# One step of a linked chain to a block of products, and its small products queued behind that block

## The chip, the core and the metric

The kernel runs on one core of a Trainium2 chip. The metric is the device time of one execution in microseconds (us), from runs of the whole program; a separate execution is recorded by the hardware profiler. A core has five engines with instruction queues of their own: TensorE (PE: matrix products and transposes; its weight loads are listed apart as PEld), VectorE (DVE), ScalarE (ACT), GpSimd (POOL) and SyncE (SP), which issues most of the transfers here. Products land in PSUM, from where VectorE and ScalarE read them. The profile also shows the clock that TensorE was granted, as a share of full speed.

## What is computed

One layer of a hybrid sequence model on a float32 input of 2048 positions by 1024 channels, with 16 learned positions put in front (T = 2064). Three groups of heads read one common projection; a gated feed-forward part follows. Cut to what matters:

```python
p = rms_norm(h, norm_mix_pre) @ w_in                  # (T, 1024) @ (1024, 3080)
oa = rg_lru_group(...)                                # linear recurrence, 256 channels
ob = forgetting_attention_group(...)                  # 8 heads of 64, causal softmax with decay
oc = rwkv7_group(...)                                 # 4 heads of 64, matrix-valued state
h = h + rms_norm(concat([oa, ob, oc]) @ w_out, norm_mix_post)
f = causal_dwconv(rms_norm(h, norm_ffn_pre) @ ffn_up, ffn_conv)
gate, val = split(f, 2)
h = h + rms_norm((gelu(gate) * val) @ ffn_down, norm_ffn_post)

# rwkv7_group, at each position, for each head:
s_kk = S @ kk_t
S = S * w_t - outer(s_kk, kk_t * a_t) + outer(v_t, k_t)
o_t = S @ r_t
```

The last three lines are the recurrence that the change is about. The kernel computes it in chunks of 64 positions: within a chunk the dependence of the positions on each other is a triangular 64 x 64 system, whose inverse is built up from 16 x 16 blocks to 32 x 32 and to 64 x 64 by small products; only one 64 x 64 state a head passes from chunk to chunk.

## The kernel before

**Stages.** The first stage makes the input projection (L226 w_in_step): each operand is split into a high and a low part, and `mm3` (L172) adds three products for each of 8 slices of the 1024 channels, so that one *block of products* is 24 products, of 128 output columns by 256 to 400 positions. The positions are taken in three parts of two blocks each; in every part 24 groups of 128 columns are gone through, thus 48 blocks of products a part and 144 in all, after a small product for the attention gates at the head of each part. Attention, the output projection, the feed-forward up projection and the down projection follow.

**Work beside the blocks.** The LRU group and the RWKV recurrence are written as Python generators, and the main loop calls `beside.advance()` (L2171) after each block of products, which traces some of their steps there. `Beside` (L2040) adds PACE = 1.25 to what is due at each call, and takes steps until less than one is due: one step a block, two after every fourth. The generators begin after the 26th block of the first part, and a third of their work is added in each part at the same place. What is left when the first stage ends is traced without any blocks (`finish`), while attention follows.

**Steps of the recurrence.** `recurrences` (L2070) goes through 9 blocks of 256 positions (the last has 64), three in each part. For each: four steps of preparation, in `block` and the head of `chunks` (L1112) (decays, keys, scores, transposes); then the triangular solve of the 16 x 16 blocks, 15 alternations of GpSimd and VectorE; then the *ending* of the block before it; then four steps of `lru_block` (L1412). An ending has ten steps:

1. load the solved 16 x 16 blocks (`xt`) and transpose them (`xr`);
2. u1: products of the scores with `xr`, masked by VectorE (L1212);
3. x1: products of `xt` with u1, added up by VectorE (L1219), and further products for the diagonal 32 x 32 blocks (L1226);
4. u2: products of the scores with x1, copied by VectorE (L1233);
5. `xf`: products with u2, copied by ScalarE (L1238);
6. to 10. products for the 64 x 64 systems (L1244, L1254), the state from chunk to chunk (L1269 to L1293), the outputs (L1320, L1325) and their norm, and the output (L1345), which is stored for the next stage.

Steps 2 to 5 are linked: each product needs what VectorE made of the product before. All of the four use the helper `small` (L1201), whose name stands in the trace as L1202: 32 x 32 products. A float32 product of this kind shows as two instructions in the trace. For a block of four chunks u1 has 64 of them, x1 32 (and 64 for the diagonal blocks), u2 32 and `xf` 32. The products of the recurrence take turns in two PSUM buffers (`rps`), those of the preparation and of the LRU group share one more (`eps`), and the blocks of products have five (`psp`).

**What sets the order.** Every engine works through its own queue in order. The order in these queues is fixed when the program is built: a scheduler goes through the traced instructions with a simulated clock, and an instruction that was traced earlier goes first among those that it holds to be ready. `tc.issue_after(i)` puts the instructions traced under it behind instruction `i` in the queue of its engine; it makes no wait of its own.

Of the kernel before, what the change touches and what calls it, by code (L numbers as in the profile page):

```python
# [20 lines left out]
KD = D // P  # L21
# [150 lines left out]
def mm3(nc, out, ah, al, bh, bl, first, last, more=False):  # L172

    nc.tensor.matmul(out, ah, bh, start=first, stop=False, skip_group_check=more)  # L174
    nc.tensor.matmul(out, ah, bl, start=False, stop=False, skip_group_check=more)  # L175
    nc.tensor.matmul(out, al, bh, start=False, stop=last, skip_group_check=more)  # L176

# [48 lines left out]
def w_in_step(core, pools, psum, weights, block, kind, c0, scr):  # L226

    nc = core.nc
    wh, wl = weights
    st = pools["st"]  # L230
    t0, n, tl, hi, lo = block
    ps = psum.tile([P, 512], F32, tag="mm", name=core.n("psp"))
    for k in range(KD):
        mm3(nc, ps[:, :n], wh[:, k], wl[:, k], hi[:, k], lo[:, k], k == 0, k == KD - 1)
    if kind in ("q", "k"):
        sc = 0.125 if kind == "q" else 1.0
# [209 lines left out]
class Attn:  # L446
# [537 lines left out]
class Rwkv:  # L984
# [3 lines left out]
    BLOCKS = 9  # L988
    SOLVED = "solved"

    @staticmethod
# [120 lines left out]
    def chunks(self, b, nch, sg, rav, bk, wc, bon):  # L1112
# [3 lines left out]
        nc, k, core = self.nc, self.k, self.core  # L1116
# [4 lines left out]
        sc = self.t([P, ni, 192], "sc", bufs=2)  # L1121
# [71 lines left out]
        nc.vector.transpose(xr.rearrange("p i s -> p (i s)"), xt.rearrange("p i s -> p (i s)"))  # L1193
        yield

        xf = self.t([64, ni, 64], "xf")
        nc.gpsimd.memset(xf[32:64, :, 0:32], 0.0)
        groups = [(i0, min(16, ni - i0)) for i0 in range(0, ni, 16)]
        m1 = k["mask1"][:].rearrange("p (o t) -> p o t", o=1)

        def small(o, lhsT, rhs, lo_out, lo_in):  # L1201
            nc.tensor.matmul(  # L1202
                o[lo_out : lo_out + 32], lhsT[lo_in : lo_in + 32], rhs[lo_in : lo_in + 32], start=True, stop=True,
                tile_position=(lo_in, lo_out),
            )

        for i0, m in groups:
            ps = self.ps().rearrange("p (i t) -> p i t", t=32)
            for i in range(m):
                for q in (0, 32):  # L1210
                    small(ps[:, i], sc[:, i0 + i, 128 + q : 160 + q], xr[:, i0 + i], q, q)
            tt(u1[:, i0 : i0 + m], ps[0:64, :m], m1.to_broadcast([64, m, 32]), op=ALU.mult)  # L1212
        yield
        for i0, m in groups:
            g = slice(i0, i0 + m)
            ps = self.ps().rearrange("p (i t) -> p i t", t=32)
            for i in range(m):
                small(ps[:, i], xt[:, i0 + i], u1[:, i0 + i], 0, 0)
            tt(x1[0:32, g], ps[0:32, :m], xr[0:32, g], op=ALU.add)  # L1219
            ps = self.ps().rearrange("p (i t) -> p i t", t=32)  # L1220
            for i in range(m):
                for q in (0, 32):
                    small(ps[:, i], u1[:, i0 + i], xt[:, i0 + i], q, q)
            for q in (0, 32):
                qs = slice(q, q + 32)
                tt(xf[qs, g, q : q + 32], ps[qs, :m], xt[qs, g], op=ALU.add)  # L1226
        yield
        for i0, m in groups:
            g = slice(i0, i0 + m)
            ps = self.ps().rearrange("p (i t) -> p i t", t=32)  # L1230
            for i in range(m):
                small(ps[:, i], sc[:, i0 + i, 160:192], x1[:, i0 + i], 32, 0)
            nc.vector.tensor_copy(u2[32:64, g], ps[32:64, :m])  # L1233
            yield
# [4 lines left out]
        yield  # L1239
        for i0 in range(0, ni, 8):  # L1240
# [6 lines left out]
            nc.scalar.activation(w3[0:64, i0 : i0 + m, 64:128], ps[0:64, :m], AF.Copy)  # L1247
        yield
        ap = self.t([P, 2, ni, 64], "xu")[0:64, 0]
        for i0 in range(0, ni, 4):  # L1250
# [5 lines left out]
            nc.scalar.activation(w3[0:64, i0 : i0 + m, 0:64], ps[0:64, :m, 64:128], AF.Copy)  # L1256
        yield
        gt, rp = self.t([P, m2, CH], "gt"), rav[:, :, 0]
# [26 lines left out]
        for c in range(nch):  # L1285
# [7 lines left out]
            nc.vector.tensor_copy(st[:, c + 1], gain[:, c])  # L1293
        yield

# [42 lines left out]
        tt(on.rearrange("p q a (h t) -> p (q a) h t", h=2), v4(od), r14, op=ALU.mult)  # L1338
        yield
        n = CH * nch  # L1340
# [20 lines left out]
        )  # L1361
        yield

# [675 lines left out]

class Beside:  # L2040


# [6 lines left out]
    def step(self):  # L2049
        while self.gens:  # L2050
            try:
                next(self.gens[0])
                return True
            except StopIteration:
                self.gens.pop(0)
        return False

    def advance(self):
        self.due += self.pace if self.gens else 0.0
        while self.due >= 1.0:  # L2060
            self.due -= 1.0
            if not self.step():
                break
# [316 lines left out]
```

## Time and profile before

| | |
|---|---|
| median of three runs | 2995.25 us (2985.94 to 2998.46) |
| profiled execution | 2996.0 us, its recorded span 2994.3 us |
| granted TensorE clock, mean | 0.976 |
| block products (L174 to L176 on psp) | 3 x 1152, 1136.6 us busy |
| TensorE's work on the recurrence's buffers (rps), 42 to 878.5 us | 161.1 us (2897 instructions) |
| the same, 878.5 to 1125 us | 82.1 us (1266 instructions) |
| waits of GpSimd for VectorE in the solve (L1178) | 67.5 us, 99 times |

Busy time of TensorE is the time in which at least one product runs; products overlap, so the sum over groups can be above it. A line such as `L1202 ... rps<-rwxu,rwsc 32*32 32x32 f32 x32 [1.46 <-DVE rwxu L1219]` gives start, duration, engine, source line, what is written from which tiles, the shape of the stationary and of the moving operand, a count of merged instructions, and in brackets the idle time of the engine before it and whose result ended it. In a list of waits the numbers are the total, how often, and the longest. The stretches that a table of windows shows are cut from the start of the span.

### The profile page before, as it was taken

What the parts mean: (1) busy time and instruction counts of PE and PEld (TensorE: products, weight loads), DVE (VectorE), ACT (ScalarE), POOL (GpSimd) and SP (SyncE); (2) the same over time, 40 slices, a digit from 0 to 9 for tenths busy, and PEclk for the clock granted to TensorE, in tenths of its full rate; (3) what the DMA queues carried; (4) which work ended last, traced back from release to release, by engine and by line L of the source; (5) the groups of instructions that cost most, each with busy time, mean ns of one, the idle gap of its engine ahead of it and who ended that gap; (6) DMA issues with size and microseconds to landing.
All of it is one profiled execution on the core that took longest, in us unless ns stands there. A gap on an engine that the chain in (4) does not pass through costs nothing.

```text
span 2994.3 us, 52802 instructions
## 1 busy us (share of the span) xinstructions
PE 2898.0 (97%) x18694; PEld 2486.3 (83%) x18694; DVE 2037.0 (68%) x3937; ACT 1480.8 (49%) x2858; POOL 1319.7 (44%) x1567
## 2 busy tenths in 40 slices
PE   6999999999999999999999999999999999999998
PEld 6998899888886655665568999999999999787887
DVE  5258644765677776565636998898778787656766
ACT  4246332443346554455634656666565665424333
POOL 1002122121223665666843667446655544656443
PEclk9999899999988999999999999999999999999999
DMA  6777469676644347544336565577777764436453
GB/s 210 239 235 226 135 230 310 203 242 194 199 129 101 95 109 208 134 113 109 77 96 212 183 198 179 173 220 211 208 208 218 222 198 128 158 116 220 145 174 120
DMA packets 469190, 530.49 MB, mean 177 GB/s; under 512 B 85710, under 2 KB 355736, under 8 KB 467372
## 3 DMA queue, kind: packets, MB, share of 16 engines
q1 hardware_dynamic: 468156, 526.17, 58.2%
q8 instruction: 147, 2.41, 0.3%
q0 software_dynamic: 768, 0.93, 0.1%
q14 instruction: 119, 0.97, 0.1%
HBM read 368.07 MB, written 158.90 MB: 176 GB/s over the span
## 4 chain that ended last, share of the span: by engine, by line
PE 59%; DVE 4%; POOL 2%; DMA 2%; ACT 2%; issue 2%; SPq 0%; DVEq 0%; POOLq 0%; ACTq 0%
PE psu L174 9%; PE psu L175 9%; PE psu L176 9%; PE po L716 4%; PE psd L174 4%; PE psd L175 4%; PE psd L176 4%; PE mx L566 2%; PE pswo L174 2%; PE pswo L176 2%; PE pswo L175 2%; PE sc L693 2%; PE sc L694 2%; POOL acc L737 1%; DVE mc L571 1%
## 5 line engine op out<-in xcount | busy, mean ns | idle before, releaser
L175 PE MATMUL psu<-xo,uw 128*128 128x344 f32 x1848 | 591.4, 320 | 0.0
L174 PE MATMUL psu<-xo,uw 128*128 128x344 f32 x1848 | 586.0, 322 | 2.7 <-ACT u L1828 1.2
L176 PE MATMUL psu<-xo,uw 128*128 128x344 f32 x1848 | 581.9, 320 | 1.3 <-POOL uw L1657 1.0
L174 PE MATMUL psp<-xh,wh 128*128 128x384 f32 (+2 forms) x1152 | 380.8, 331 | 0.0
L176 PE MATMUL psp<-xh,wl 128*128 128x384 f32 (+2 forms) x1152 | 378.0, 328 | 0.0
L175 PE MATMUL psp<-xl,wh 128*128 128x384 f32 (+2 forms) x1152 | 377.8, 328 | 0.0
L1657 DVE TENSOR_TENSOR uw<-uq,uw 128x512 fp32r<-128x512 f32 x341 | 320.3, 944 | 59.2 <-ACT uw L1656 56.7
L174 PEld LDWEIGHTS psu<-xo,uw 128*128 128x128 f32 x1848 | 345.8, 188 | 4.3 <-DVE vb L1848 1.8
L176 PEld LDWEIGHTS psu<-xo,uw 128*128 128x128 f32 x1848 | 345.7, 188 | 2.1 <-POOL uw L1657 1.3
L175 PEld LDWEIGHTS psu<-xo,uw 128*128 128x128 f32 x1848 | 347.1, 188 | 0.0
L1656 ACT ACTIVATE uw<-uq 128x512 fp32r<-128x512 f32 x462 | 287.9, 627 | 95.7 <-PE psu L176 44.4
L698 ACT ACTIVATE p<-sc,bias 128x512 f32<-128x512 f32 (+4 forms) x352 | 197.9, 590 | 142.3 <-PE sc L694 119.2
L571 DVE TENSOR_REDUCE mc<-mx 128x1 f32<-128x512 f32 (+6 forms) x352 | 190.0, 565 | 113.6 <-PE mx L566 80.1
L1796 DVE SCALAR_TENSOR_TENSOR uy<-psu,ffn_cols,uy 128x342 f32<-128x342 f32 (+1 forms) x390 | 220.4, 567 | 61.4 <-ACT uy L1794 59.7
L1804 POOL TENSOR_TENSOR uy<-uy,uy 128x342 f32<-128x342 f32 (+1 forms) x132 | 146.5, 1110 | 229.2 <-DVE uy L1796 55.9
L737 POOL TENSOR_TENSOR acc<-acc,p 128x512 f32<-128x512 f32 (+3 forms) x208 | 222.7, 1073 | 48.4 <-DVE acc L737 23.4
L1657 POOL TENSOR_TENSOR uw<-uq,uw 128x512 fp32r<-128x512 f32 x121 | 184.4, 1524 | 133.8 <-ACT uw L1656 116.0
L174 PEld LDWEIGHTS psp<-xh,wh 128*128 128x128 f32 x1152 | 220.1, 191 | 8.7 <-issue 7.3
L176 PEld LDWEIGHTS psp<-xh,wl 128*128 128x128 f32 x1152 | 220.1, 191 | 7.0 <-issue 5.1
L175 PEld LDWEIGHTS psp<-xl,wh 128*128 128x128 f32 x1152 | 220.1, 191 | 5.0 <-issue 3.2
L1657 DVE TENSOR_TENSOR fo<-u,fo 128x896 fp32r<-128x896 f32 x88 | 101.6, 1155 | 133.7 <-ACT fo L1656 133.2
L1656 ACT ACTIVATE fo<-u 128x896 fp32r<-128x896 f32 x88 | 81.2, 923 | 206.6 <-PE psd L176 118.1
(488 smaller groups left out, 6409.4 us busy)
## 6 DMA issues: line engine op xcount, KB each, us to landing
uq<-scr_us SPq DMA_DIRECT2D x220, 256.0 KB
uq<-in_ffn_up_dram SPq DMA_DIRECT2D x209, 256.0 KB
wl<-scr_wk SPq DMA_DIRECT2D x48, 512.0 KB
wh<-scr_wk SPq DMA_DIRECT2D x48, 512.0 KB
u<-scr_ff SPq DMA_DIRECT2D x88, 256.0 KB
scr_ff<-uy SPq DMA_DIRECT2D x110, 171.0 KB
raw<-in_w_in_dram SPq DMA_DIRECT2D x24, 512.0 KB
scr_wk<-wh SPq DMA_DIRECT2D x24, 512.0 KB
```

The lines of the kernel that those rows point to most:

```text
L174: nc.tensor.matmul(out, ah, bh, start=first, stop=False, skip_group_check=more)
L175: nc.tensor.matmul(out, ah, bl, start=False, stop=False, skip_group_check=more)
L176: nc.tensor.matmul(out, al, bh, start=False, stop=last, skip_group_check=more)
L566: nc.tensor.matmul(ps[:rows, : e - a], q3[:, qo : qo + rows], k2[:, a:e], start=True, stop=not last)
L571: self.reduced = nc.vector.tensor_reduce(mc[:rows, i, ci : ci + 1], ps[:rows, : e - a], axis=AX.X, op=ALU.max)
L698: last = nc.scalar.activation(p[:rows, :w], ps[:rows, :w], AF.Exp, bias=bias[:rows, j : j + 1])
L716: mm = nc.tensor.matmul(po[at : at + 64, c0:n], v1[:rows, j], p[:rows, : n - c0], start=start and i < 2, stop=end and i + 2 >= len(group), ...
L737: eng.tensor_tensor(a, ps_[0][0][:rows, c0:n] if start and i == 1 else a, p[:rows, : n - c0], op=ALU.add)
L1656: core.nc.scalar.activation(hi, src, AF.Copy)
L1657: (eng or core.nc.vector).tensor_tensor(lo, src, hi, op=ALU.subtract)
L1796: core.conved = stt(y[:, :n], src[:, i : n + i], cw[:, 44 * i + cc : 44 * i + cc + 1], y[:, :n], op0=ALU.mult, op1=ALU.add)
L1804: core.pooled = nc.gpsimd.tensor_tensor(v[:, :n], g[:, :n], v[:, :n], op=ALU.mult)
```

## The change

The generators' ending returns a mark, FAR, at each of its yields. `advance` takes at most two steps at a call, and stops after a step that returned the mark. The three linked products u1, x1 and u2 are put behind the last product of the block of products that was traced before them; for that, `mm3` returns its last instruction and `w_in_step` keeps it. No instruction is added or removed on any engine. The other nine places where a plain `yield` becomes `yield self.FAR` are left out.

```diff
@@ mm3
-    nc.tensor.matmul(out, al, bh, start=False, stop=last, skip_group_check=more)
+    return nc.tensor.matmul(out, al, bh, start=False, stop=last, skip_group_check=more)
@@ w_in_step
-        mm3(nc, ps[:, :n], wh[:, k], wl[:, k], hi[:, k], lo[:, k], k == 0, k == KD - 1)
+        core.produced = mm3(nc, ps[:, :n], wh[:, k], wl[:, k], hi[:, k], lo[:, k], k == 0, k == KD - 1)
@@ class Rwkv
     SOLVED = "solved"
+    FAR = "far"
@@ chunks
         nc.vector.transpose(xr.rearrange("p i s -> p (i s)"), xt.rearrange("p i s -> p (i s)"))
-        yield
+        yield self.FAR
...
+        behind = lambda: core.tc.issue_after(core.produced.ins)
...
                 for q in (0, 32):
-                    small(ps[:, i], sc[:, i0 + i, 128 + q : 160 + q], xr[:, i0 + i], q, q)
+                    with behind():
+                        small(ps[:, i], sc[:, i0 + i, 128 + q : 160 + q], xr[:, i0 + i], q, q)
...
             for i in range(m):
-                small(ps[:, i], xt[:, i0 + i], u1[:, i0 + i], 0, 0)
+                with behind():
+                    small(ps[:, i], xt[:, i0 + i], u1[:, i0 + i], 0, 0)
...
             for i in range(m):
-                small(ps[:, i], sc[:, i0 + i, 160:192], x1[:, i0 + i], 32, 0)
+                with behind():
+                    small(ps[:, i], sc[:, i0 + i, 160:192], x1[:, i0 + i], 32, 0)
...
@@ class Beside
+    MOST = 2
...
     def step(self):
         while self.gens:
             try:
-                next(self.gens[0])
-                return True
+                return next(self.gens[0]) or True
             except StopIteration:
                 self.gens.pop(0)
         return False

     def advance(self):
         self.due += self.pace if self.gens else 0.0
-        while self.due >= 1.0:
+        for _ in range(self.MOST):
+            if self.due < 1.0:
+                break
             self.due -= 1.0
-            if not self.step():
+            if self.step() in (False, Rwkv.FAR):
                 break
```

More of the change, by code (lines that the diff above doesn't have):

```diff
@@ L1210, in chunks @@
                 for q in (0, 32):
-                    small(ps[:, i], sc[:, i0 + i, 128 + q : 160 + q], xr[:, i0 + i], q, q)
+                    with behind():
+                        small(ps[:, i], sc[:, i0 + i, 128 + q : 160 + q], xr[:, i0 + i], q, q)
             tt(u1[:, i0 : i0 + m], ps[0:64, :m], m1.to_broadcast([64, m, 32]), op=ALU.mult)
-        yield
+        yield self.FAR
         for i0, m in groups:
@@ L1226, in chunks @@
                 tt(xf[qs, g, q : q + 32], ps[qs, :m], xt[qs, g], op=ALU.add)
-        yield
+        yield self.FAR
         for i0, m in groups:
@@ L1231, in chunks @@
             for i in range(m):
-                small(ps[:, i], sc[:, i0 + i, 160:192], x1[:, i0 + i], 32, 0)
+                with behind():
+                    small(ps[:, i], sc[:, i0 + i, 160:192], x1[:, i0 + i], 32, 0)
             nc.vector.tensor_copy(u2[32:64, g], ps[32:64, :m])
-            yield
+            yield self.FAR
             ps = self.ps().rearrange("p (i t) -> p i t", t=32)
@@ L1238, in chunks @@
             nc.scalar.activation(xf[0:32, g, 32:64], ps[0:32, :m], AF.Copy)
-        yield
+        yield self.FAR
         for i0 in range(0, ni, 8):
@@ L1247, in chunks @@
             nc.scalar.activation(w3[0:64, i0 : i0 + m, 64:128], ps[0:64, :m], AF.Copy)
-        yield
+        yield self.FAR
         ap = self.t([P, 2, ni, 64], "xu")[0:64, 0]
@@ L1256, in chunks @@
             nc.scalar.activation(w3[0:64, i0 : i0 + m, 0:64], ps[0:64, :m, 64:128], AF.Copy)
-        yield
+        yield self.FAR
         gt, rp = self.t([P, m2, CH], "gt"), rav[:, :, 0]
@@ L1293, in chunks @@
             nc.vector.tensor_copy(st[:, c + 1], gain[:, c])
-        yield
+        yield self.FAR
         ntl = -(-nch // 2)
@@ L1338, in chunks @@
         tt(on.rearrange("p q a (h t) -> p (q a) h t", h=2), v4(od), r14, op=ALU.mult)
-        yield
+        yield self.FAR
         n = CH * nch
@@ L1361, in chunks @@
         )
-        yield
+        yield self.FAR
 def lru_consts(core, pool, psum, w):
```

## The prediction

> **What bounds the kernel now.** I read the page first (engines, clock row), then the stretches of the first stage, then TensorE's waits there, then the instructions around the longest of them. Columns of the stretches: bounds and length, then busy us (count) of TensorE, its weight loads, VectorE, ScalarE and GpSimd, the granted clock, DMA share, GB/s.
>
> ```profile
> span 2994.3 us, 52802 instructions
> PE 2898.0 (97%) x18694; PEld 2486.3 (83%) x18694; DVE 2037.0 (68%) x3937; ACT 1480.8 (49%) x2858; POOL 1319.7 (44%) x1567
> PEclk9999899999988999999999999999999999999999
> ```
>
> TensorE is the bound, over the whole span. What the change can win is TensorE's idle time and the time at a lowered clock; it removes no product.
>
> ```profile
> 42.00:878.50 836.50, 820.16 (x6809) 755.60 (x6808) 488.42 (x1181) 338.58 (x647) 140.53 (x218) 0.97 0.67 214
> 878.50:1125.00 246.50, 227.67 (x1982) 154.37 (x1983) 185.44 (x514) 137.78 (x297) 131.87 (x206) 0.86 0.45 106
> 289.60:317.00 27.40, 25.70 (x253) 20.88 (x246) 24.18 (x70) 17.28 (x33) 9.69 (x14) 0.50 0.25 83
> 405.70:412.60 6.90, 6.54 (x47) 6.47 (x48) 3.51 (x8) 0.00 (x0) 0.32 (x1) 0.51 0.10 30
> 671.90:678.80 6.90, 6.49 (x49) 4.97 (x50) 6.53 (x15) 3.62 (x8) 2.36 (x5) 0.51 0.42 133
> 767.50:771.00 3.50, 3.50 (x20) 3.47 (x17) 2.94 (x8) 1.00 (x4) 0.50 (x1) 0.51 0.65 186
> 317.00:878.50 561.50, 551.02 (x5121) 502.71 (x5120) 333.93 (x831) 215.16 (x425) 116.91 (x179) 0.98 0.66 213
> ```
>
> Blocks of products run from 42 to 878.5 us. There TensorE idles 836.5 - 820.2 = 16.3 us, and the clock is 0.97. From 878.5 to 1125 the recurrence's rest runs beside attention: 18.8 us idle, clock 0.86. The half-speed stretches inside the first stage are the four small ones above (among others): one where the first third of the stage meets the second (289.6 to 317), and three of 6.9, 6.9 and 3.5 us.
>
> ```profile
> PE rps L1202 <- DVE rwxu L1219: 6.1, 4, 2.5
> PE pst L145 <- DVE xl L152: 2.0, 1, 2.0
> 401.49 2.21 PE L1202 MATMUL rps<-rwxu 32*32 32x32 f32 x96
> 406.06 1.91 PE L1202 MATMUL rps<-rwxu,rwsc 32*32 32x32 f32 x32 [1.46 <-DVE rwxu L1219]
> 407.90 0.69 PE L174 MATMUL psp<-xh,wh 128*128 128x384 f32 x1
> 408.39 0.52 PE L175 MATMUL psp<-xl,wh 128*128 128x384 f32 x1
> ...
> 412.73 0.34 PE L174 MATMUL psp<-xh,wh 128*128 128x384 f32 x1
> 412.91 0.33 PE L175 MATMUL psp<-xl,wh 128*128 128x384 f32 x1
> ...
> 563.88 1.19 PE L1202 MATMUL rps<-rwxu,rwsc 32*32 32x32 f32 x32 [0.38 <-DVE rwxu L1219]
> 672.31 1.91 PE L1202 MATMUL rps<-rwxu,rwsc 32*32 32x32 f32 x32 [2.47 <-DVE rwxu L1219]
> 766.41 1.19 PE L1202 MATMUL rps<-rwxu,rwsc 32*32 32x32 f32 x32 [1.80 <-DVE rwxu L1219]
> 859.14 1.19 PE L1202 MATMUL rps<-rwxu,rwsc 32*32 32x32 f32 x32
> ```
>
> The largest wait of the stage after 302 us is the linked chain: the product u2 (the 32 recorded instructions with rwsc) needs the sum x1 that VectorE makes (L1219) from the product ahead of it. It waits four times, in blocks 1 to 4 of the recurrence, 1.46, 0.38, 2.47 and 1.80 us; in block 5 (859.14) it doesn't. Each of the three long ones opens one of the half-speed stretches: the block products behind it take 0.52 us (start to start 0.32) against 0.34 (0.175) further on.
>
> ```profile
> 403.45 0.75 DVE L1458 TENSOR_TENSOR_SCAN rwlu<-rwla,lru_h,rwlg 128x256 f32<-128x256 f32 x1
> 405.34 0.67 DVE L1219 TENSOR_TENSOR rwxu<-rps,rwxu 32x512 f32<-32x512 f32 x1
> 408.10 0.67 DVE L1233 COPY rwxu<-rps 32x512 f32<-32x512 f32 x1
> ```
>
> Why is x1 late? Its product starts at 401.49, its sum only at 405.34: VectorE works through the LRU group's steps (L1458 and its neighbours) first.
>
> **The change part by part.** mm3 now returns its last product, and w_in_step keeps it as core.produced: no instruction, 0 us. Beside.step hands on the value FAR, advance takes at most MOST = 2 steps, and none after one that returned FAR. With 1.25 steps due at each block of products, before, each fourth block took two; I counted both orders through by hand, from block of products 26, where the recurrence begins, to 144, the last. After a FAR step the debt is carried (up to 3.0 steps) and paid back in the LRU and the next block's front, two steps at a time. Both orders leave the same 28 steps over at the end of the stage, so the work behind 878.5 us is the same. Of the three linked products u1, x1, u2 of a block of the recurrence, only these stood two to a block of products: u1 and x1 of block 1, x1 and u2 of blocks 3 and 5. The LRU steps move one or two blocks of products later (block 2's from 58-60 to 60-61, block 4's from 99-101 to 101-102). No DMA is added; the transfers in the steps (xt's loads, the store of mix) move with them by at most three blocks of products on SP's queue.
>
> The second part queues u1 (64 recorded instructions), x1 (32) and u2 (32) behind the last product traced before them. What does that hold back? I compare where each stood when it was traced with where it ran, by the block products that had started by then (24 to a block).
>
> ```profile
> 42.00:395.90 353.90, 272.74 (x1448) 258.18 (x1448) 20.02 (x36) 18.98 (x39) 0.96 0.66 213
> 42.00:552.60 510.60, 399.31 (x2101) 373.58 (x2101) 31.59 (x57) 26.31 (x54) 0.96 0.71 230
> 42.00:659.70 617.70, 464.70 (x2478) 430.65 (x2478) 37.80 (x69) 31.27 (x65) 0.97 0.70 227
> 42.00:756.40 714.40, 525.01 (x2920) 486.20 (x2920) 41.57 (x78) 34.65 (x74) 0.97 0.69 222
> 42.00:848.50 806.50, 585.85 (x3348) 540.88 (x3348) 48.67 (x95) 38.83 (x85) 0.97 0.68 219
> ```
>
> These stretches count block products alone, up to the start of u1 of blocks 1 to 5: 1448/24 = 60.3, 87.5, 103.3, 121.7 and 139.5 blocks. Traced they are after 51, 79, 94, 106 and 128. So u1 runs 8 to 16 blocks of products later than its place in the program, because the chain of the recurrence (each step waits for a PSUM buffer and for VectorE) is slower than the pace. A rule that holds it behind block 51 (or x1 behind 52 instead of 51) binds nothing at block 60. I cost the queueing at 0; the cover that hides it is this lag, and without it a linked product would be at most one block later: 24 products at the 0.175 us start to start seen above, 4.2 us.
>
> Does splitting the pairs shorten the waits? The trace holds the answer in part: block 4's three products are already traced one to a block (106, 107, 108), as the change wants, and its u2 still waits 1.80 us and is followed by 3.5 us at half clock; block 5's x1 and u2 are a pair and u2 doesn't wait at all. What is late next after x1 is VectorE's queue, not the order of TensorE's. Bounds: at most all of it goes, 6.1 us of waits and half of the stretches of 6.9 + 6.9 + 3.5 us, 8.6: 14.7 us won. On the other side, each of some 15 linked products before 878.5 us (three in each of five blocks) comes 4.2 us later, 63 us of chain that run behind 878.5 instead. What does a us of chain cost there? The tail loses 18.8/246.5 = 0.08 to idling and 0.14 to the clock, the stage from 317 on 0.02 and 0.02: 0.18 more. 63 x 0.18 = 11 us lost. Between these I take the row nearest to a split trio, block 4: a wait of 1.8 and half of 3.5, 3.5 us. Block 1 (1.46 + 3.45 = 4.9) and block 3 (2.47 + 3.45 = 5.9) come down to that: 1.4 + 2.4, about 4 us won.
>
> The stretch from 289.6 to 317 I leave as it is. The blocks of the first third are done by then and the norms of the second third feed no products yet, so there is no block for the recurrence's products to stand behind. The LRU steps moved by a block or two run beside blocks that keep TensorE busy; were they to meet the next linked sum on VectorE, they cost one more wait like the four, 0.4 to 2.5 us.
>
> The Trainium skill, "TensorE: Matmul & The Clock Gate", section "Why this matters for your kernels", puts the loss of the clock at idle gaps beyond some 3 us between bursts. Here the clock halves after gaps of 1.46, 2.47 and 1.80 us with sparse 32x32 products around them, so the trace is stricter than the rule. By the rule the change could win only the 6.1 us of waits, by the rows up to 14.7.
>
> The sum: the profiled execution took 2996.0 us, 1.7 beyond its span of 2994.3; 2996.0 - 4 = 2992. It lies 0.7 us above the median of the three times shown (2995.25), so against that I forecast **2991**.
>
> **The rivals.** *It works as it says* (2978): a whole block then stands between two linked products wherever the stage has blocks, the four waits and their half-speed stretches go (14.7), and the small products beyond 302 us at the first seam, spread likewise, give back half of what the half clock costs between 302 and 317, a quarter of 15 us (about 3.5). 18 us in all, from 2996.0. For it: each long wait opens a half-speed stretch, so one cause takes both. Against it: the lag of 8 to 16 blocks, and block 4.
>
> *The chain falls back* (3013): u1, x1 and u2 are held until a block has been issued, VectorE's LRU work meets them there, and a whole period of the recurrence (u1 of block 4 to u1 of block 5 is 848.5 - 756.4 = 92 us) slides behind 878.5. At 0.18 us each us that is 17 us, 2996.0 + 17. It decides from 15/0.18 = 83 us of added chain, some 14 us or three and a half blocks in each of six periods. For it: the tail is the worst place for this chain, clock 0.86. Against it: the same 28 steps are left over, and the queueing is slack.
>
> *It doesn't do what it says*: the order on TensorE comes out the same and the time stays at 2995; this lies inside my own case.
>
> **How the numbers follow.** My forecast with the unchanged order 0.44, 2991, own range 2984 to 2999. It works: 0.36. The chain falls back: 0.20. What a measurement here can tell from no change is about 0.5%, 15 us: faster means below 2980, slower above 3010. Nearly all of the second case lies below (0.34 with what strays), the third above but for a little, together with mishaps of the first 0.21; within 0.45. The range reaches to the middle of both rivals and leaves out 0.1 on each side: 2974 to 3012.
>
> **What would show it.** The recurrence's last transposes stand so far in this row (their first and last start):
>
> ```profile
> L1345 PE MATMUL rps<-ident,rwxu x2: 364/365/366, 1119.5 to 1121.4; 64*128 64x64 f32 x2
> ```
>
> Right: u1 of block 1 still near 60 blocks of products, waits of L1202 for L1219 of 4 to 6 us in the stage, clock 0.97 there, those transposes still near 1121 us. Wrong on the fast side: those waits below 1 us and a clock of 0.99 beyond 317 us. Wrong on the slow side: more than 83 us of the recurrence's chain moved past the last block, or a stage that ends later than 878.5. The forecast rests on the lag; if a changed place in the program changes the order of the engines' queues more widely, it fails there.

## The result, and the profile after

The changed kernel takes 3005.37 us (median of nine runs, 2999.9 to 3012.64). The kernel before, run beside it, takes 2994.27 us (nine runs, 2985.94 to 3000.02). The ratio is 1.0041 with a 95% interval of 1.0029 to 1.0053: 0.41% slower. The forecast, 2991 us, lay on the other side; the range, 2974 to 3012, holds the time.

The page of the changed kernel, in the first two rows that were shown of before:

```profile
span 3010.9 us, 52805 instructions
PE 2902.7 (96%) x18694; PEld 2489.5 (83%) x18694; DVE 2029.8 (67%) x3937; ACT 1484.6 (49%) x2858; POOL 1320.1 (44%) x1567
```

TensorE is busy for 4.7 us more with the same 18,694 instructions. The profiled execution took 3012.64 us, the longest of the nine runs; that of before took 2995.96, near its median. So 16.7 us are to be found between the two, of which some 11 are typical.

Stretches of the changed kernel (columns as in the prediction). The first has the bounds that were used for before. The others are cut at its own marks: from the first block product to the start of the 55th block of products, from there to the last block product, from there to the recurrence's last product, and from there to attention's last product (`po`).

```profile
42.00:878.50 836.50, 819.33 (x6797) 755.87 (x6796) 482.56 (x1177) 340.19 (x646) 142.37 (x220) 0.97 0.66 214
...
41.77:354.77 313.00, 307.62 (x2045) 287.95 (x2045) 175.79 (x405) 132.00 (x237) 26.00 (x45) 0.97 0.66 211
354.77:876.62 521.85, 510.06 (x4744) 466.63 (x4743) 305.66 (x770) 207.56 (x408) 114.82 (x174) 0.97 0.67 217
...
876.60:1134.30 257.70, 229.59 (x1998) 155.79 (x1997) 187.25 (x514) 137.84 (x297) 128.62 (x204) 0.86 0.42 100
1134.30:1554.10 419.80, 405.88 (x1833) 238.75 (x1832) 245.07 (x489) 212.99 (x386) 287.39 (x374) 0.98 0.46 117
```

The same marks in the kernel before:

```profile
42.15:361.46 319.31, 313.45 (x2045) 292.88 (x2045) 175.93 (x406) 130.33 (x236) 27.95 (x45) 0.95 0.65 208
361.46:877.96 516.50, 506.02 (x4763) 462.26 (x4763) 312.23 (x776) 208.21 (x411) 112.58 (x173) 0.98 0.68 219
...
878.00:1121.90 243.90, 225.52 (x1977) 153.27 (x1977) 184.43 (x507) 135.18 (x293) 130.80 (x205) 0.86 0.45 106
1121.90:1538.40 416.50, 404.24 (x1833) 237.86 (x1833) 245.29 (x490) 213.97 (x388) 287.04 (x375) 0.98 0.47 118
```

The reader is to see that the first stage did not get longer in these two executions (its last block product starts at 876.6 instead of 878.0 us), but that two changes of opposite sign hide in this: the changed kernel gains 6.3 us up to the 55th block of products, at the seam of the first two thirds, and loses 5.4 from there to the last. The stretch in which the rest of the recurrence runs beside attention got longer: 257.7 - 243.9 = 13.8 us, of which TensorE idles 28.1 - 18.4 = 9.7 more. Attention behind it took 3.3 us more, and what follows attention is equal within 1 us. The work left behind the stage is the same: TensorE is busy on the recurrence's buffers for 82.25 us after the last block product, before 82.26.

Inside the stage, the longest of TensorE's waits, the products u2 of blocks 1 to 5, four of which wait for x1 (now L1205 and L1224; the lines of the ending stand 3 to 6 lower than before), and the recurrence's last transposes:

```profile
PE rps L1205 <- DVE rwxu L1224: 8.8, 4, 3.5
```

```profile
403.94 1.35 PE L1205 MATMUL rps<-rwxu,rwsc 32*32 32x32 f32 x32 [2.75 <-DVE rwxu L1224]
558.00 1.66 PE L1205 MATMUL rps<-rwxu,rwsc 32*32 32x32 f32 x32 [1.19 <-DVE rwxu L1224]
669.82 1.91 PE L1205 MATMUL rps<-rwxu,rwsc 32*32 32x32 f32 x32 [3.49 <-DVE rwxu L1224]
766.13 1.61 PE L1205 MATMUL rps<-rwxu,rwsc 32*32 32x32 f32 x32 [1.36 <-DVE rwxu L1224]
...
865.17 1.35 PE L1205 MATMUL rps<-rwxu,rwsc 32*32 32x32 f32 x32
```

```profile
L1351 PE MATMUL rps<-ident,rwxu x2: 364/365/366, 1130.2 to 1132.9; 64*128 64x64 f32 x2
```

The waits that a split was to shorten grew: 1.46, 0.38, 2.47 and 1.80 us became 2.75, 1.19, 3.49 and 1.36, in sum 8.8 for 6.1. Two more executions with the order of before have 6.7 (e1) and 7.8 us (e5), one more with the order of the change 11.1 (e6); up to the end of the stage the queues of these are the same as in the pair.

For blocks 2 and 3 the reason stands in TensorE's order. So many block products are queued between the start of x1 and the start of u2:

| block of the recurrence | 1 | 2 | 3 | 4 | 5 |
|---|---|---|---|---|---|
| before | 4 | 16 | 18 | 2 | 16 |
| with the change | 4 | 4 | 6 | 3 | 16 |

The rule traces x1 and u2 one block of products (24) apart in all five, but the queue has 3 to 6 between them in the first four, fewer than before. One block apart in the program is not one block apart in the queue: the scheduler places these products 8 to 16 blocks of products later than they were traced, by its own clock. So TensorE has less to do while VectorE makes the sum. At block 1 the count is the same; there the sum itself starts 5.1 us after x1 (398.08 us) instead of 3.9, with VectorE at LRU steps until then. Executions spread here too: with the order of before, e1 and e5 wait 2.21 and 2.10 us at block 1, not 1.46.

What VectorE does in that time also changed at the longest wait, block 3. Here are the four engines around it in the changed kernel: SyncE's issue of an LRU load, ScalarE, VectorE, TensorE.

```profile
662.96 0.47 SPq L1432 DMA_DIRECT2D rwlraw<-scr_p  x1
...
667.27 0.60 ACT L1439 ACTIVATE rwlu<-rwlraw,lru_cols 128x256 f32<-128x256 f32 x1 [4.52 <-DMA rwlraw<-scr_p]
...
669.18 0.42 ACT L1462 ACTIVATE rwlr<-rwlr 128x256 f32<-128x256 f32 x1
...
667.91 0.51 DVE L1441 SCALAR_TENSOR_TENSOR rwlu<-rwlraw,lru_cols,rwlu 128x256 f32<-128x256 f32 x1 [4.40 <-ACT rwlu L1439]
669.09 0.67 DVE L1224 TENSOR_TENSOR rwxu<-rps,rwxu 32x512 f32<-32x512 f32 x1
...
661.71 2.21 PE L1205 MATMUL rps<-rwxu 32*32 32x32 f32 x96
```

The product x1 starts at 661.71 and takes 2.21 us, but its sum L1224 runs only at 669.09. VectorE isn't busy for most of it: it stands still for 4.40 us at the head of its queue, at an LRU instruction that needs ScalarE, and ScalarE stands still for 4.52 us at an LRU load that was issued at 662.96. The linked sum is queued behind both. ScalarE in the kernel before, at the same two instructions:

```profile
663.46 0.42 ACT L1456 ACTIVATE rwlr<-rwlr 128x256 f32<-128x256 f32 x1
...
665.92 0.60 ACT L1433 ACTIVATE rwlu<-rwlraw,lru_cols 128x256 f32<-128x256 f32 x1
```

The instruction that waits (L1433, now L1439) is the first of the LRU group's block 5. It is traced only after some 115 blocks of products, but the scheduler holds it ready and puts it here, near block 104. Before, it stood behind the square root that ends block 4's gates (L1456, now L1462), and its load, issued at 661.29, had landed when it was due. The rule traces block 4's LRU steps two blocks of products later (their first gate products run at 646.34 instead of 640.54 us); so block 5's first instruction now stands ahead of block 4's square root, and the 4.3 us from its load's issue to its start lie open.

That this order made the wait longer is not shown here. The product x1 of the kernel before, and u2 of the same block in e5, which has the order of before:

```profile
664.25 2.21 PE L1202 MATMUL rps<-rwxu 32*32 32x32 f32 x96
...
670.04 1.19 PE L1202 MATMUL rps<-rwxu,rwsc 32*32 32x32 f32 x32 [3.49 <-DVE rwxu L1219]
```

Before, u2 started 672.31 - 664.25 = 8.06 us after x1, with the change 669.82 - 661.71 = 8.11: the sum was as late, behind other work of VectorE, and only TensorE had more to do (18 block products instead of 6). In e5 the wait is 3.49 us as well, without the rule. And over the whole kernel the first instructions of the LRU blocks (L1433, now L1439) wait for transfers 35.7 us in 15 cases, before 33.0 in 12.

A wait of the same kind stands behind the stage. TensorE, then ScalarE in the changed kernel:

```profile
909.17 0.79 PE L693 MATMUL sc<-q,k 128*128 128x512 f32 x1 [5.56 <-ACT p L698]
...
908.62 0.35 ACT L1026 ACTIVATE rwwa<-rwraw,rwkv_om 128x64 f32<-128x64 f32 x1 [5.78 <-DMA rwraw<-scr_p]
908.87 0.25 ACT L698 ACTIVATE p<-sc,bias 16x16 f32<-16x16 f32 x1
```

and ScalarE at that instruction in the kernel before:

```profile
905.45 0.35 ACT L1025 ACTIVATE rwwa<-rwraw,rwkv_om 128x64 f32<-128x64 f32 x1 [1.58 <-DMA rwraw<-scr_p]
```

An exponential of attention (L698) stands behind a preparation step of the recurrence's last block, whose operand is read back from memory. ScalarE waits 5.78 us for it instead of 1.58, and TensorE 5.56 us for the exponential: the longest single wait between 877 and 1134 us. In this stretch TensorE's waits for exponentials make 6.9 us instead of 3.3; those for attention's maxima from VectorE (L571, L576) grew more, to 11.2 from 4.0.

### The profile page after: what moved, and what is told of

The parts are those of the page before. It is cut to its first block, busy times and chain, and to the rows that moved or that the text cites. A ratio compares the mean times of both kernels' runs of the same rounds, so it can differ in the third digit from the quotient of the medians.

```text
span 3010.9 us, 52805 instructions
## 1 busy us (share of the span) xinstructions
PE 2902.7 (96%) x18694; PEld 2489.5 (83%) x18694; DVE 2029.8 (67%) x3937; ACT 1484.6 (49%) x2858; POOL 1320.1 (44%) x1567
## 4 chain that ended last, share of the span: by engine, by line
PE 76%; DVE 8%; DMA 6%; ACT 3%; POOL 3%; issue 2%; SPq 1%; DVEq 0%; POOLq 0%; ACTq 0%
PE psu L174 9%; PE psu L175 8%; PE psu L176 8%; PE psp L175 5%; PE psp L176 5%; PE psp L174 5%; PE psd L174 4%; PE psd L175 4%; PE psd L176 4%; PE po L716 4%; PE mx L566 2%; PE pswo L174 2%; PE pswo L175 2%; PE pswo L176 2%; PE sc L693 2%
## 5 line engine op out<-in xcount | busy, mean ns | idle before, releaser
L698 ACT ACTIVATE p<-sc,bias 128x512 f32<-128x512 f32 (+4 forms) x352 | 198.1, 591 | 153.6 <-PE sc L694 127.8
L571 DVE TENSOR_REDUCE mc<-mx 128x1 f32<-128x512 f32 (+6 forms) x352 | 190.1, 565 | 118.4 <-PE mx L566 81.7
```

The source lines that it names most:

```text
L571: self.reduced = nc.vector.tensor_reduce(mc[:rows, i, ci : ci + 1], ps[:rows, : e - a], axis=AX.X, op=ALU.max)
L698: last = nc.scalar.activation(p[:rows, :w], ps[:rows, :w], AF.Exp, bias=bias[:rows, j : j + 1])
```

## The experiments

Each kernel computes the whole layer. Ratios are against the kernel before, run on the same chip, five rounds each. The letters of the theories are those of the moment: in e1 A says that the queueing is free, in e2 to e4 that the loss follows how far the chain has come at the end of the stage, in e6 that it arises only where recurrence and attention interleave; the others say what they mean in place.

**The queueing alone (e1).** The new rule is taken out of `advance`, the three `issue_after` stay.

```diff
-        for _ in range(self.MOST):
-            if self.due < 1.0:
-                break
+        while self.due >= 1.0:
             self.due -= 1.0
-            if self.step() in (False, Rwkv.FAR):
+            if not self.step():
                 break
```

> The queueing of u1, x1 and u2 alone, with the old rule for steps (as many as are due). Theory A (the queueing binds nothing, since these products run 8 to 16 blocks of products after their place in the program): ratio 1.000, within 0.1%, and every queue as before. Rival Q (the queueing costs): about 1.004, as with the whole change.

Measured: 1.000 [0.9987, 1.0013]. As built, the queues of all five engines are row for row those of the kernel before; with the rule but no queueing they are those of the changed kernel. What was costed at 0 is 0, and all that follows is about the rule in `advance`.

**The rule in a part of the stage (e2, e3), and three steps instead of two (e4).** `part` is the third of the stage.

```diff
-        for _ in range(self.MOST):
+        for _ in range(self.MOST if self.part < 2 else 9):
...
-            if self.step() in (False, Rwkv.FAR):
+            if self.step() in ((False, Rwkv.FAR) if self.part < 2 else (False,)):
```

In e3 it is `self.part == 2`; in e4 only `MOST = 3`.

> The rule of one marked step to a block in the first two thirds of the stage only, the old rule in the last; queueing left in. Counted out of the program's queues, u1 of block 5 of the recurrence then stands behind 140.2 blocks of products (before 139.5, after the change 140.6). Theory A (the loss follows how far the chain has come when the last block of products ends, some 10 us for one block of products): 0.7 later, +7 us, ratio 1.002. Rival B (the tail beside attention is reshuffled, with no relation to the chain's place): anywhere from 0.996 to 1.004. Rival C (the splitting itself costs where it is done, most of it in the first two thirds): 1.003 to 1.004.

> The rule of one marked step to a block in the last third of the stage only. u1 of block 5 stands behind 139.3 blocks of products, 0.2 earlier than before. Theory A: -2 us, ratio 0.999. Rival B: anywhere from 0.996 to 1.004. Rival C: 1.001 at most, as only the pairs of blocks 4 and 5 are split.

> The whole change, but with three steps at most to a block instead of two (debt paid back faster). u1 of block 5 stands behind 140.6 blocks of products, as with the change. Theory A: as the change, ratio 1.004. Rival B: anywhere from 0.996 to 1.004. Rival C: 1.004.

Measured: e2 1.0024 [1.0008, 1.0041], e3 1.000 [0.9985, 1.0014], e4 1.0015 [1.0003, 1.0027]. The rule alone in the last third costs nothing, though its steps stand nearest there to the stretch that lost the time; in the first two thirds it costs 0.24%. The two don't add up to 0.41%, but the intervals leave room for that. e4 refutes A and C: the chain stands where it does with the change (140.6), the splits are the same, and yet the loss is 0.15% instead of the 0.4% that both gave it. No part wins anything.

**The two apart (e5, e6).** A barrier for all engines behind the recurrence keeps attention from starting beside it, in the kernel before and in the changed one.

```diff
         rec.close()
+        tc.strict_bb_all_engine_barrier()
```

> The kernel before with a barrier of all engines between the end of the recurrence and the start of attention: the rest of the recurrence runs alone. Both theories: much slower than before, some 60 to 130 us (ratio 1.02 to 1.045), since attention no longer runs beside it. It is the base for the next run.

> The changed kernel with the same barrier. Theory A (the loss arises only where the rest of the recurrence and attention share the engines' queues): against the run before with the barrier the 11 us shrink to what the chain is behind at the end of the stage, one block of products, less what the stage gains: 0 to +4 us, 0.000 to 0.0015 in the ratio. Rival D (the loss lies in attention itself, in the order of its own loads and queues, or in the stage): it stays at 9 to 13 us, 0.003 to 0.0045 in the ratio.

Measured: e5 1.0295 [1.0276, 1.0313], e6 1.0346 [1.0328, 1.0364]. The difference of 0.0051 remains although nothing interleaves any more, against A and for D, and is above D's 0.0045 too. Stretches of e5: the stage, then attention from the recurrence's last product to attention's own last product, then 295 us of it from shortly before the first `sc` product.

```profile
39.50:873.80 834.30, 818.20 (x6806) 754.17 (x6805) 487.59 (x1181) 338.75 (x646) 139.84 (x218) 0.97 0.67 215
1043.30:1625.40 582.10, 534.66 (x2507) 314.86 (x2506) 336.76 (x704) 303.49 (x572) 395.85 (x540) 0.97 0.51 125
1055.00:1350.00 295.00, 264.38 (x1298) 153.12 (x1296) 175.10 (x389) 157.71 (x306) 189.53 (x272) 0.96 0.65 157
```

The same three of e6:

```profile
40.60:878.20 837.60, 817.57 (x6787) 754.05 (x6786) 485.13 (x1175) 339.40 (x643) 139.46 (x218) 0.97 0.67 214
1050.00:1648.00 598.00, 545.90 (x2506) 319.88 (x2506) 335.51 (x704) 303.65 (x573) 394.31 (x540) 0.94 0.50 121
1062.00:1357.00 295.00, 260.80 (x1215) 147.52 (x1214) 165.14 (x365) 148.94 (x291) 173.29 (x252) 0.91 0.59 145
```

Attention's instructions are the same (2506), and no line of attention was changed; yet it takes 598.0 us instead of 582.1, at a clock of 0.94 instead of 0.97. Its waits for VectorE's maxima from 1055 to 1660 us, in e5:

```profile
PE mx L566 <- DVE mc L571: 4.6, 12, 0.9
PE mx L579 <- DVE sh L576: 3.1, 6, 0.9
```

and in e6:

```profile
PE mx L566 <- DVE mc L571: 6.8, 14, 2.1
PE mx L579 <- DVE sh L576: 4.7, 7, 2.0
```

Single waits reach 2.1 and 2.0 us instead of 0.9, and the clock in the first 295 us is 0.91 instead of 0.96. What differs as built is the order: behind the recurrence, some 1,080 of TensorE's 2,608 rows stand elsewhere in e6.

**Another pace (e7, e8).** Is that the doing of the rule, or does any shift of the steps reshuffle the order behind them?

```diff
-PACE = 1.25
+PACE = 1.24
```

> The kernel before, with nothing of the change, at a pace of 1.24 steps instead of 1.25. u1 of block 5 stands behind 140.2 blocks of products (before 139.5), and the recurrence's rest reaches further into attention (its last output stands behind 319 of attention's score and value products, before 308). If the loss of the change has nothing to do with linked steps and is only the place of the chain in the tail: 3 to 10 us slower, ratio 1.001 to 1.0035. If it comes with the splitting: 1.000.

> The kernel before at a pace of 1.30. u1 of block 5 stands behind 139.6 blocks of products, the last output behind 293 of attention's products (before 308). Place of the chain in the tail: 0 to 5 us faster, ratio 0.998 to 1.000. Otherwise 1.000.

Measured: at 1.24 1.0066 [1.0048, 1.0084], at 1.30 1.0028 [1.0015, 1.0041], both above what was expected. A pace 1% lower, without the rule, costs more than the whole change.

**Order or rule, held apart (e9 to e12).** Attention's order in the kernels with the barrier falls into two groups: that of e5, and that of e6. These four kernels cross them with the rule. All have the barrier; e9 and e10 have the rule as in e2 and e3, e11 has no rule and PACE = 1.20, e12 the whole change and PACE = 1.35.

> The new rule in the first two thirds of the stage, and attention held back behind the recurrence. Read from the engines' queues as built: behind the recurrence, attention's order on TensorE, VectorE and ScalarE is row for row that of the kernel before held apart (e5), while that of the change held apart (e6) differs from it in some 1,080 of TensorE's 2,608 rows. Theory O (the loss is in attention's order as the scheduler happens to put it, not in the moved steps): like e5, ratio 1.025 to 1.031, and from the recurrence's last product to attention's last 580 to 586 us as in e5 (582), granted clock near 0.97 there. Theory S (the moved steps themselves cost, whatever the order behind them): between e5 and e6, 1.031 to 1.034, and near 593 us.

> The new rule in the last third alone, and attention held back. This rule alone cost nothing in the kernel as it is (e3, ratio 1.000). Its attention order held apart is that of the change (e6) but for 8 of TensorE's 2,608 rows. Theory O: like e6, ratio 1.033 to 1.036, and 594 to 602 us from the recurrence's last product to attention's last, clock 0.94. Theory S: like e5, 1.028 to 1.031, 582 us, since the rule in the last third cost nothing.

> No new rule at all: the kernel before, held apart, with 1.20 steps due at each block of products instead of 1.25. TensorE's attention order is row for row that of e10. Theory O: the loss appears without the change: 594 to 602 us from the recurrence's last product to attention's last, clock 0.94 there, ratio 1.034 to 1.039 (a few us more recurrence are left behind the stage). Theory S: 582 us there, ratio 1.029 to 1.033.

> The whole change, held apart, with 1.35 steps due at each block of products instead of 1.25. TensorE's and ScalarE's attention order is row for row that of the kernel before held apart (e5). Theory O: the loss is gone with the whole change in: 579 to 586 us from the recurrence's last product to attention's last, clock 0.97 there, ratio 1.024 to 1.031. Theory S: 594 to 602 us as in e6, ratio 1.031 to 1.036.

Measured: e9 1.0293 [1.0274, 1.0312], e10 1.034 [1.0324, 1.0357], e11 1.0337 [1.0321, 1.0352], e12 1.0318 [1.0302, 1.0334]. Attention in each, in this order (one row of each kernel's stretches):

```profile
1044.90:1627.10 582.20, 537.54 (x2506) 316.88 (x2507) 336.39 (x704) 303.41 (x573) 394.66 (x540) 0.96 0.51 125
```

```profile
1040.90:1634.00 593.10, 542.88 (x2507) 317.56 (x2507) 333.91 (x704) 303.63 (x573) 394.35 (x540) 0.95 0.50 122
```

```profile
1037.70:1630.60 592.90, 540.20 (x2506) 317.14 (x2507) 335.49 (x704) 303.61 (x573) 394.35 (x540) 0.95 0.50 122
```

```profile
1051.10:1631.30 580.20, 536.00 (x2506) 316.15 (x2506) 336.40 (x704) 303.67 (x573) 394.65 (x540) 0.96 0.51 125
```

With the order of e5 attention takes 582.2 us (rule in two thirds) and 580.2 (whole change); with the other order 593.1 (rule in the last third) and 592.9 without any rule. So the loss inside attention belongs to its order, which a shift of the steps by other means tips as well, and the rule is not needed for it. e10 and e11 came 1 us below the bound that had been set for attention, and e11 as a whole just below its own (1.0337, bound 1.034). e12 came out above its bound as a whole (1.0318, bound 1.031): attention was as expected, the stage was not, as the last pair shows.

**Does the rule have a price of its own? (e13 to e16)** The change and the kernel before at three more paces, without the barrier: e13 and e14 are the pairs to e7 and e8, e15 and e16 a pair of their own.

> The whole change with 1.24 steps due at each block of products. The kernel before at this pace (e7) stood at 1.0066. Theory S (the new rule costs about 0.4% whatever the order around it): 1.009 to 1.012. Theory O (each build is one reshuffling of the order beside attention, and the rule has no price of its own there): anywhere from 0.999 to 1.007, and no nearer to 1.0107 than another; not above 1.008.

> The whole change with 1.30 steps due. The kernel before at this pace (e8) stood at 1.0028. Theory S: 1.005 to 1.008. Theory O: anywhere from 0.999 to 1.007; TensorE's order beside attention resembles that of e2 (1.0024) most, so near 1.002.

> The kernel before with 1.20 steps due, the pair to e16. Both theories: 0.999 to 1.007, with the last block product 1 to 5 us earlier and that much more of the recurrence behind it.

> The whole change with 1.20 steps due. Theory S: 0.003 to 0.005 above e15. Theory O: the difference to e15 has no fixed sign; over the four pairs (paces 1.20, 1.24, 1.25, 1.30) the differences spread by more than 0.004, and at least one of them is at or below zero.

| steps due at a block | before | with the change | difference |
|---|---|---|---|
| 1.20 | 1.0021 [1.0008, 1.0035] | 1.0064 [1.0040, 1.0087] | 0.0043 |
| 1.24 | 1.0066 [1.0048, 1.0084] | 1.0119 [1.0098, 1.0140] | 0.0053 |
| 1.25 | 1 | 1.0041 [1.0029, 1.0053] | 0.0041 |
| 1.30 | 1.0028 [1.0015, 1.0041] | 1.0055 [1.0036, 1.0074] | 0.0027 |

Theory O, "one reshuffling of many", falls for the kernel as it is: each pair has the same sign, and four differences between 0.0027 and 0.0053 spread by 0.0026, no more than their intervals (some 0.0025 to either side). The rule costs 0.3 to 0.5% at each of the four paces. e15's last block product came later than before (880.1 us), not 1 to 5 us earlier as both theories had it. These profiles are weak ground for placing the price: they are single executions, and those of e8 and e15 were 11 to 12 us above their medians, that of e16 11 us below.

**Where it is paid (e17, e18).** Two pairs with the barrier and with one attention order in each pair: e17 (the change at 1.20) to e11, and e18 (before at 1.35) to e12.

> The whole change, held apart, 1.20 steps due: the pair to e11 (1.0337), whose attention order on all five engines it shares. Theory M (the price is paid only where the recurrence's rest and attention share the queues): equal to e11 within 0.002, 1.032 to 1.0355, attention 593 us as there. Theory S2 (the moved steps cost in the stage or in the recurrence's rest itself): 1.0365 to 1.039, attention 593 us, with the 12 us in the stage or behind it.

> The kernel before, held apart, 1.35 steps due: the pair to e12 (1.0318), with the same attention order on TensorE and ScalarE. Theory M: 1.030 to 1.0335, stage near e12's 842 us. Theory S2: 1.026 to 1.029, stage or recurrence's rest 9 to 13 us shorter than e12's 842 and 168 us.

Measured: e17 1.0345 [1.0321, 1.037], to e11's 1.0337; e18 1.0279 [1.0253, 1.0305], to e12's 1.0318. e18 has these rows for the stage, for 60 us of it, and for attention:

```profile
41.20:869.60 828.40, 812.72 (x6787) 749.58 (x6785) 485.03 (x1174) 338.41 (x644) 141.60 (x218) 0.98 0.67 216
760.00:820.00 60.00, 58.53 (x595) 52.72 (x595) 36.45 (x95) 17.92 (x43) 10.01 (x15) 0.97 0.60 188
1037.90:1618.30 580.40, 536.62 (x2506) 316.49 (x2505) 335.84 (x704) 304.06 (x572) 395.49 (x540) 0.96 0.52 125
```

and e12, with the change, the first two:

```profile
40.90:882.80 841.90, 823.36 (x6786) 759.98 (x6785) 483.20 (x1175) 339.13 (x644) 139.34 (x218) 0.96 0.66 213
760.00:820.00 60.00, 56.04 (x615) 49.71 (x615) 35.68 (x94) 20.05 (x44) 12.33 (x19) 0.89 0.57 180
```

At 1.35 attention is equal (580.4 and 580.2) and the difference of 0.0039 lies in the stage: 841.9 - 828.4 = 13.5 us with the same instructions, 2.9 of them idle, the rest products at a lower clock (0.96 for 0.98). The worst place, ScalarE, VectorE and TensorE of e12:

```profile
760.50 0.60 ACT L1439 ACTIVATE rwlu<-rwlraw,lru_cols 128x256 f32<-128x256 f32 x1 [2.50 <-DMA rwlraw<-scr_p]
...
762.41 0.42 ACT L1462 ACTIVATE rwlr<-rwlr 128x256 f32<-128x256 f32 x1
...
761.13 0.48 DVE L1441 SCALAR_TENSOR_TENSOR rwlu<-rwlraw,lru_cols,rwlu 128x256 f32<-128x256 f32 x1 [1.60 <-ACT rwlu L1439]
764.72 0.65 DVE L1216 TENSOR_TENSOR rwxu<-rps,rmask 64x512 f32<-64x512 f32 x1
...
765.63 3.59 PE L1205 MATMUL rps<-rwxu 32*32 32x32 f32 x96 [3.96 <-DVE ccol L431]
```

The mask in the kernel without the rule, e18:

```profile
754.83 0.67 DVE L1212 TENSOR_TENSOR rwxu<-rps,rmask 64x512 f32<-64x512 f32 x1
```

It is the order shown in the changed kernel, one block of the recurrence later: the next LRU block's first instruction ahead of the square root, ScalarE waiting for its load, VectorE for ScalarE, the mask of u1 (L1216) behind them. Here the pair shows the delay: the mask starts 8.8 us after u1 (755.88 us), in e18 3.8 us after it (751.00). x1 waits 3.96 us (L431, which the row names, is the small copy behind L1216 on VectorE). The clock of the 60 us around it is 0.89 for 0.97. The rest of the 13.5 us stands elsewhere in the stage and was not taken apart. At 1.20 the pair differs by 0.0008, within its intervals; the profiled stage is 839.0 us with the change and 832.2 without. So theory M falls at 1.35, where e18 came out in S2's range; at 1.20 the ratio is in M's range and below S2's 1.0365.

The cut at the 55th block of products can be made in all seven profiled pairs with and without the rule. From there to the last block product the kernel with the rule takes 5.3 to 17.7 us longer in six of them, and 5.0 us less in the seventh (1.20 without the barrier); up to there it lies between 6.3 us ahead and 1.8 behind. With the rule in the first two thirds alone this stretch isn't longer than before (e2 515.9, e9 514.9 us, before 516.5); what lengthens it in the others stays open.

None of the 18 kernels that were run is faster than the kernel before; e1 and e3 are equal to it.

## Why the prediction was wrong, point by point

- **Queueing costs 0:** right (e1, 1.000). The lag that hides it is there: u1 of block 1 starts at 392.4 us after 1458 block products, 60.8 blocks, predicted near 60.
- **The work left behind the stage is the same, and the chain hardly moves:** right (82.25 and 82.26 us; u1 of block 5 at 140.6 blocks of products for 139.5). With it the rival "The chain falls back" is refuted as a mechanism, though its 3013 had the right sign: about one block of products, some 5 us, was moved, not 83.
- **Stage clock 0.97, a stage that doesn't end later than 878.5:** right for the profiled pair. At 1.35 steps, held apart, the stage got 13.5 us longer.
- **The split wins about 4 us:** wrong, and the first step that failed. "Between these I take the row nearest to a split trio, block 4": the prediction counted the splits where the steps are traced ("x1 and u2 of blocks 3 and 5") and let blocks 1 and 3 "come down to" block 4's wait. In the queue there was no split: 3 to 6 block products stand between x1 and u2 of blocks 1 to 4, where 24 were meant and 2 to 18 stood before, and the waits grew (8.8 for 6.1 us). The prediction held the reason in its hand, the lag of 8 to 16 blocks, and block 4, whose u2 waits 1.80 us although it is traced one to a block. It used the lag for the queueing and not for the split. The rival "It works as it says" asks for a whole block between two linked products, and fails by the same count.
- **The first seam stays as it is:** wrong, to the other side. The 55th block of products starts 313.0 us after the first with the change and 319.3 before, 6.3 us gained (5.6 in the pair e5 and e6).
- **The LRU steps moved by one or two blocks cost nothing:** wrong at 1.35 steps, open at 1.25. The text named them and priced them at nothing, as running "beside blocks that keep TensorE busy", with 0.4 to 2.5 us should they meet a linked sum. Delayed, they were overtaken by the first instruction of the LRU block behind them, which waits for its load and holds up ScalarE, VectorE and the linked product in turn (2.50, 1.60 and 3.96 us in e12, against a pair without it). At 1.25 the same chain is there (4.52, 4.40 and 3.49), but the sum was as late without it.
- **Equal work behind 878.5 costs equal time:** wrong, and the largest term of the profiled pair. With equal work it lost 13.8 us beside attention and 3.3 behind; e1, with the queues of before, took 241.5 us between the marks where before took 243.9 and the change 257.7. Held apart, attention's order alone is worth 11 to 18 us (580.2 to 582.2 us in four kernels with the one order, 592.9 to 598.0 in four with the other). The prediction's last sentence named this as the place where it could fail, but gave it no price and no chance.

Shown are thus: the queueing is free; the rule does not put more products between x1 and u2; it costs 0.3 to 0.5% at four paces; at 1.35 steps an LRU instruction that waits for its load at the head of ScalarE's queue delays a linked product; attention's order, tipped by other shifts of the steps as well, is worth as much as the whole effect. Left open is why the price has the same sign at four paces, and how it divides: at 1.25 the profiled pair has it behind the stage, at 1.35 the pair has it in the stage, and single executions differ by as much as what is looked for. It was not tried to move the LRU's loads ahead of the steps that use them.

## What to carry to other kernels

Where a scheduler orders the queues, the spacing at which steps are traced is not the spacing at which they run: count in the queue as built what stands between two linked products, before their waits are priced (here 3 to 6 products instead of the 24 that were meant). When steps are spread more evenly, ask of every step that moves with them what may now overtake it, and what that waits for: an instruction that reads back from memory, put early into an engine's queue, can hold up that engine, the next one and the linked chain in turn (in e12 by 2.50, 1.60 and 3.96 us). A change of a few steps can reorder work a long way behind; measure it at several neighbouring settings (here four paces) before its price or its gain is believed, and use a barrier to hold stages apart when the place of a loss is in question. Don't place an effect of 0.4% by one profiled execution of each kernel when runs of one kernel spread by as much.

## What was not expected of the hardware

The recurrence's rest by itself, in e5 between the last block product and its own last product, and 15 us of it:

```profile
873.80:1043.30 169.50, 126.06 (x1304) 105.14 (x1303) 89.26 (x293) 48.26 (x108) 18.60 (x39) 0.50 0.06 14
990.00:1005.00 15.00, 15.00 (x127) 14.46 (x125) 4.87 (x14) 3.27 (x7) 5.25 (x8) 0.50 0.02 4
```

TensorE is busy for 74% of it and never leaves half clock (0.50; 0.50 to 0.56 in all eight kernels held apart), not even over 15 us in which the trace shows no idle time of it. Beside attention the same work stands in a stretch with 0.86. And where attention's order got worse, idle time was the smaller part: of the 15.9 us between e5 and e6, 4.7 are idle (52.1 for 47.4), and 11.2 are the same 2506 instructions taking longer (545.90 for 534.66), at a clock of 0.94 for 0.97.
